# Gather operations issued from inside the mixer's step loop, with four more row buffers lent until the spread starts

## The chip, the cores and the metric

The kernel runs on one core of a Trainium2 chip. The metric is the device time of one execution in microseconds (us), given as the median of several runs. PE is the matrix engine (TensorE), DVE the vector engine, ACT the scalar engine, POOL is GpSimd, which here mainly issues indirect DMAs, and SP is the sync engine, which issues most plain DMAs.

## The reference

One layer of a decoder, 1024 tokens of 1024 channels: a mixer of three branches, then a feed-forward layer of product-key experts (PEER), then a norm.

```python
h = rms_norm(x, norm_mix)
proj = h @ w_in          # columns for the three branches and for the merge gates
o_sb  = stick_breaking_attention(...)     # 8 heads x 64, strictly causal
o_nsa = nsa_attention(...)                # compressed, selected and sliding branch
o_hg  = hgrn2_recurrence(...)             # 4 heads, chunks of 64
m = gm[0] * (o_sb @ w_sb) + gm[1] * (o_nsa @ w_nsa) + gm[2] * (o_hg @ w_hg)
x = x + m @ w_out

xc = rms_norm(x, norm_ffn)                # PEER, per token
qh = (xc @ w_q).reshape(T, 8, 2, 64)
s = einsum("nhad,akd->nhak", qh, sub_keys)        # 2 x 128 keys
top_s, top_i = top_k(s, 16)
best_s, pos = top_k(all 16 x 16 sums of top_s, 16)
eidx = ...                                # 8 heads x 16 of 16384 experts for each token
gate = softmax(best_s)
hpre = einsum("nd,nhkd->nhk", xc, u_tab[eidx])
act  = gate * gelu(hpre)
x = x + einsum("nhk,nhkd->nd", act, v_tab[eidx])
out = rms_norm(x, norm_final)
```

Each token needs 128 rows of u_tab and 128 rows of v_tab, each of 1024 float32.

## The kernel before, in words

**Parts.** The tokens are cut into four parts of 256. The mixer goes through them in order. It is written by a loop of steps (`while t < N + 3 or todo`). A step writes a few items of the three branches and then as many "pieces" (projections, gates, tails, routing) as keep PE's and VectorE's estimated work even; `mark()` closes it. `mark` stores the last VectorE instruction that has been written and the estimates v and p, in us, of the VectorE and PE work of the step.

**Two ways through PEER.** Parts 1 and 2 (`DENSE`) go through all 16384 experts with matmuls, after the mixer: 128 blocks of 128 experts each, whose u and v rows are read in full. Each token's gate for each expert comes from the spread: `spread_pieces` builds one-hot rows (`hot`, VectorE), multiplies them (`gb`, PE) and evicts the product with ACT into a staging tile of 128 x 128 x 16 float32, from which ACT's queue stores it to `d_G`. Two of the three staging tiles are the two halves of `stages`, 2 x 8 KB of each partition.

Parts 0 and 3 go through gathers. They are four tiles of 128 tokens. `gather_tile` does for each of its tiles: load of the tile's h2 row, indices and gates; 128 times an indirect DMA on POOL's queue (L1149, one u row for each of the 128 partitions, 512 KB) and a VectorE operation that multiplies it with h2 and sums it into a column of `hpre` (L1151, `u`); gelu; load of the residual row into `gacc`; 128 times an indirect DMA of a v row (L1159) and a VectorE multiply-add into `gacc` (L1161); the last norm and the store. That makes 1024 gathers.

**Buffers.** Part 0's gathers use the buffers of tag "rows", RB = 5 of 4 KB for each partition. The h2 row takes one of them, and the `gacc` row one when its turn comes. (During part 0 of the mixer the raw weights use the same five.) Part 3's gathers add space of the mixer that is free by then (`late_rows`; `rr_u`, `rr_v` in the profile).

**What sets the order.** The program is written first, and a scheduler then orders the instructions of each engine: the ones that can run by its estimates, in order of their priority, which is the order in which they were written. In the kernel before, `gather_tile` is called at the very end of the program, behind the dense stage. So a gather is behind everything else that can run. The buffers of a tag are given out in the order in which they come free in that schedule. Two things pull the gathers forward: their DMAs go to POOL, which has little else to do, and their VectorE operations are written under `paced()`, which issues each of them right behind the VectorE instruction of a certain mark. `paced` gives 420 gathers (`PACE`) to the steps from number 135 (`PACE0`) on, in proportion to p + 3.0 (`PB`); all others come behind the last mark.

The plain loads (weights, `gacc`, `h2`) are issued by SP in one queue in order; a load that waits for its buffer holds the ones behind it.

## Time and profile before

| | before |
|---|---|
| median of 3 runs | 3502.45 us (3502.05 to 3503.18) |
| profiled execution | 3511.97 us, its span 3510.2 us |
| PE busy | 3199.7 us (91%) |
| VectorE busy | 3000.6 us (85%) |
| ACT busy | 1556.4 us (44%) |
| POOL busy | 1361.7 us (39%) |
| moved by DMA | 1058.00 MB, mean 301 GB/s |
| mean TensorE clock granted | 0.942 |
| first gather issued | 579.8 us |
| first matmul of the spread | 1216.9 us |

Busy time is the time in which an engine executed something; a share is that over the span. Where rows give "duration min/median/max, first and last start", times are in us from the start of the span and durations in ns. In the listing of waits a row names the engine, the instruction that stood idle, what released it, and then the idle time in all, the number of times and the longest, in us. Rows of DMAs give the time from issue to landing. In a row of windows "(x95)" behind a busy time counts instructions. The executions of this profile and of the timed runs are different ones: the profiled one took 9.5 us longer than the median.

### The profile page before, as it was taken

How to read it: one execution, taken by the hardware profiler on the slowest of the kernel's cores; microseconds unless marked ns; L12 is line 12 of the kernel's file. 1: busy time of each engine (PE TensorE's matmuls, PEld its weight loads, DVE VectorE, ACT ScalarE, POOL GpSimd, SP SyncE). 2: the span in 40 equal slices, each digit the busy share in tenths (PEclk: the TensorE clock that was granted, in tenths of full speed). 3: DMA queues.
4: the chain of work that ended last, by engine and by line, in shares of the span. 5: the costliest groups of instructions: out<-in, count | busy, mean ns of one | idle time of the engine just before them, and what ended most of it. 6: DMA issues, size and time to landing. Idle time of an engine off the chain costs nothing.

```text
span 3510.2 us, 56907 instructions
## 1 busy us (share of the span) xinstructions
PE 3199.7 (91%) x20564; PEld 2175.3 (62%) x20564; DVE 3000.6 (85%) x6666; ACT 1556.4 (44%) x3181; POOL 1361.7 (39%) x1170
## 2 busy tenths in 40 slices
PE   7999889999997799999887889889999999999998
PEld 6887777778886688888565745434444444444443
DVE  6665679888789879889997869999988998998998
ACT  5776455554543554554455233333333333333333
POOL 0000002443332322333231334357765565676672
PEclk9999999999997799999688999989999999999999
DMA  8964856889976588897574998789999999999995
GB/s 305 334 248 147 308 185 226 320 314 310 358 284 231 199 289 291 327 332 259 191 250 154 344 372 312 241 271 387 392 384 329 385 367 362 362 368 375 367 358 219
DMA packets 359283, 1058.00 MB, mean 301 GB/s; under 512 B 35236, under 2 KB 107573, under 8 KB 354391
## 3 DMA queue, kind: packets, MB, share of 16 engines
q0 software_dynamic: 147456, 536.94, 42.5%
q1 hardware_dynamic: 206934, 483.87, 38.7%
q10 hardware_dynamic: 4608, 33.56, 2.5%
q8 instruction: 161, 2.64, 0.3%
q14 instruction: 124, 1.01, 0.1%
HBM read 944.13 MB, written 110.10 MB: 300 GB/s over the span
## 4 chain that ended last, share of the span: by engine, by line
PE 49%; DVE 23%; DMA 11%; issue 8%; ACT 6%; POOL 2%; SPq 0%; DVEq 0%; POOLq 0%; ACTq 0%
PE g L265 13%; PE acc L1441 10%; PE pj_mg L265 4%; DVE u L1151 3%; DVE gacc L1161 3%; PE g L1441 3%; DMA u<-in_peer_u_dram,gidx 3%; PE pj_r_hg L265 2%; DMA v<-in_peer_v_dram,gidx 1%; PE pb L265 1%; DMA gt<-d_G 1%; PE pj_wo L265 1%; POOL v L1159 1%; PE z_sb L417 1%; DMA vraw<-in_peer_v_dram 1%
## 5 line engine op out<-in xcount | busy, mean ns | idle before, releaser
L1159 POOL DMA_INDIRECT v<-in_peer_v_dram,gidx x421 | 556.0, 1321 | 674.0 <-DVE gacc L1161 348.4
L1149 POOL DMA_INDIRECT u<-in_peer_u_dram,gidx x417 | 529.7, 1270 | 596.6 <-DVE u L1151 367.4
L265 PE MATMUL g<-h,us 128*128 128x512 f16 x3072 | 688.2, 381 | 14.8 <-ACT ge L1400 12.1
L1441 PE MATMUL acc<-vs,ac 128*128 128x512 f16 x2304 | 542.2, 383 | 39.9 <-ACT vs L220 23.5
L1441 PEld LDWEIGHTS <-ac 128*128 128x128 f16 x3072 | 303.1, 99 | 426.1 <-issue 66.8
L1161 DVE SCALAR_TENSOR_TENSOR gacc<-v,act,gacc 128x1024 f32<-128x1024 f32 x421 | 538.9, 1280 | 29.4 <-DMA v<-in_peer_v_dram,gidx 25.8
L265 PEld LDWEIGHTS <-us 128*128 128x128 f16 x3072 | 301.6, 98 | 383.0 <-issue 21.1
L1151 DVE SCALAR_TENSOR_TENSOR u<-u,gh 128x1024 f32<-128x1024 f32 x417 | 501.9, 1219 | 33.2 <-DMA u<-in_peer_u_dram,gidx 32.7
L1400 ACT ACTIVATE ge<-g 128x512 f32<-128x512 f32 x128 | 76.1, 596 | 520.7 <-PE g L265 500.1
L265 PE MATMUL pj_mg<-hT,w_mg 128*128 128x256 f16 x2304 | 273.8, 275 | 4.0 <-ACT mg L885 4.0
L265 PEld LDWEIGHTS <-w_mg 128*128 128x128 f16 x2304 | 228.2, 100 | 33.6 <-issue 6.6
L1441 PE MATMUL g<-vs,ac 128*128 128x512 f16 x768 | 190.5, 388 | 11.6 <-ACT ge L1400 11.6
L1149 POOL DMA_INDIRECT rr_u<-in_peer_u_dram,gidx x95 | 134.2, 1413 | 96.7 <-DVE rr_u L1151 49.8
L221 DVE SCALAR_TENSOR_TENSOR vs<-vraw,vs 128x1024 f16<-128x1024 f32 x128 | 154.1, 1219 | 18.6 <-ACT vs L220 18.5
L221 DVE SCALAR_TENSOR_TENSOR us<-uraw,us 128x1024 f16<-128x1024 f32 x128 | 156.1, 1219 | 10.4 <-ACT us L220 10.3
L265 PE MATMUL pb<-o,w_b 128*128 128x256 f16 x1152 | 144.7, 281 | 21.1 <-DVE sg L923 15.1
L1159 POOL DMA_INDIRECT rr_v<-in_peer_v_dram,gidx x90 | 123.0, 1367 | 102.2 <-DVE gacc L1161 81.4
L220 ACT ACTIVATE vs<-vraw 128x1024 f16<-128x1024 f32 x128 | 131.0, 1046 | 55.0 <-DMA vraw<-in_peer_v_dram 55.0
L220 ACT ACTIVATE ac<-ge 128x512 f16<-128x512 f32 x128 | 79.9, 628 | 168.3 <-DVE ge L1434 139.0
L1434 DVE TENSOR_TENSOR ge<-ge,gt 128x256 f32<-128x256 f32 x256 | 98.4, 422 | 58.7 <-ACT ge L1400 44.9
L1223 PE MATMUL gb<-hot 128*128 128x128 f16 x512 | 125.7, 294 | 24.3 <-ACT stage L1226 13.1
L220 ACT ACTIVATE us<-uraw 128x1024 f16<-128x1024 f32 x128 | 134.2, 1048 | 21.4 <-PE g L265 12.8
(1146 smaller groups left out, 6353.8 us busy)
## 6 DMA issues: line engine op xcount, KB each, us to landing
uraw<-in_peer_uT_dram SPq DMA_DIRECT2D x128, 512.0 KB, 7.7
vraw<-in_peer_v_dram SPq DMA_DIRECT2D x128, 512.0 KB, 7.2
w_mg<-dw SPq DMA_DIRECT2D x72, 512.0 KB, 5.8
gt<-d_G SPq DMA_DIRECT2D x32, 1024.0 KB, 17.5
d_G<-stages ACTq DMA_DIRECT2D x20, 1024.0 KB, 5.9
w_r_hg<-dw SPq DMA_DIRECT2D x36, 512.0 KB, 5.4
w_b<-dw SPq DMA_DIRECT2D x72, 256.0 KB, 5.5
wr_mg<-in_wblk_dram SPq DMA_DIRECT2D x24, 512.0 KB, 5.3
```

The costliest lines, as they stand in the source:

```text
L220: S.activation(hi, src, AF.Copy, scale=scale)
L221: V.scalar_tensor_tensor(lo, in0=src, scalar=scale, in1=hi, op0=ALU.mult, op1=ALU.subtract)
L265: P.matmul(ps, l[:, k, :], r[:, k, :], start=(i == 0), stop=(i == n - 1))
L417: P.matmul(x["z"], qz[:, hh, tl * 128:(tl + 1) * 128], st["k"][:, r0 + c0:r0 + c1], start=True, stop=(c0 > 0))
L1149: G.indirect_dma_start(out=ur, out_offset=None, in_=a["peer_u"], in_offset=bass.IndirectOffsetOnAxis(ap=idx[:, c:c + 1], axis=0))
L1151: V.scalar_tensor_tensor(ur, in0=ur, scalar=1.0, in1=h2, op0=ALU.mult, op1=ALU.mult, accum_out=hpre[:, c:c + 1])
L1159: G.indirect_dma_start(out=vr, out_offset=None, in_=a["peer_v"], in_offset=bass.IndirectOffsetOnAxis(ap=idx[:, c:c + 1], axis=0))
L1161: V.scalar_tensor_tensor(acc, in0=vr, scalar=act[:, c:c + 1], in1=acc, op0=ALU.mult, op1=ALU.add)
L1223: P.matmul(ps[:, n, :], hs[:, 0, :, n], hs[:, 2, :, n], start=True, stop=False)
L1400: S.activation(ge, ps, AF.Gelu, scale=1.0 / (SW * SH2))
L1434: V.tensor_tensor(gv, gv, gt[:, :, i % 8, :], op=ALU.mult)
L1441: P.matmul(ps, ac[:, x, t * 128:(t + 1) * 128], v[:, y, dh * 512:(dh + 1) * 512], start=start and n == 0, stop=stop and n == 2)
```

## The change

The generator `gather_rows` holds the whole list of gathers: `gather_tile` now yields behind each of them. The step loop calls `gather_due()` behind each `mark()`. From step 135 on it adds 0.19 * (p + 3.0) (the new `PACE`) to the gathers owed and writes those that have come due into the program, as soon as the routing of part 0 is written. So their priority is that of the step. Their VectorE operations stand behind the VectorE instruction of the mark just made, and the old table of `paced` is gone. `seen[0]` is moved on, so that the estimates v and p leave the gathers out. What is left of the list at the program's end is written there, as before.

`lent_rows` gives part 0's gathers their buffers: of each eight in a row, the first four take a "rows" buffer as before and the next four a quarter of `stages` (4 KB of each partition), which stands idle until the spread. The first piece of the spread sets `lent[1]`, and from then on all take "rows" buffers. The profile and the listings below show a gather in lent space under the name `stages`.

```diff
@@ -23,7 +23,7 @@
 
 RPE, RDVE, REND, PD = 3.5, 3.0, 5.0, 1.2
 
-PACE0, PACE, PB = 135, 420, 3.0
+PACE0, PACE, PB = 135, 0.19, 3.0
 
 TP, LEAD = 3, 3
 
@@ -1114,30 +1114,22 @@
         total_[:] = load_["DVE"], load_["PE"]
         marks.append((next(i for i in reversed(nc.cur_bb.bb.instructions) if i.engine == mybir.EngineType.DVE), v, p))
 
-    paces = []
-
     def paced():
 
-        if not paces:
-            def rows(tau):
-                return [tau * (p + PB) if k >= PACE0 else 0.0 for k, (_, v, p) in enumerate(marks)]
-
-            lo, hi = 0.0, 10.0
-            for _ in range(40):
-                mid = (lo + hi) / 2
-                lo, hi = (mid, hi) if sum(rows(mid)) < PACE else (lo, mid)
-            acc = 0.0
-            for m, r in zip(marks, rows(lo)):
-                acc += r
-                paces.extend([m[0]] * (int(acc) - len(paces)))
-            paces.append(marks[-1][0])
-            paces.append(0)
-        k = paces[-1]
-        paces[-1] += 1
-        return tc.issue_after(paces[min(k, len(paces) - 2)])
+        return tc.issue_after(marks[-1][0])
+
+    lent = [0, False]
+
+    def lent_rows(name):
+
+        j = lent[0] % 8
+        lent[0] += 1
+        if j < 4 or lent[1]:
+            return rows(name)
+        return stages[:, j // 2 - 2, j % 2 * 64:j % 2 * 64 + 64].rearrange("p a b -> p (a b)")
 
     def gather_tile(ti):
-        row = late_rows if ti // 2 == PARTS[-1].i else rows
+        row = late_rows if ti // 2 == PARTS[-1].i else lent_rows
         h2 = load(rows(f"gh2_{ti}"), d_h2[ti])
         idx = load(gat.tile([128, 128], I32, tag="gidx", name=f"gidx_{ti}", bufs=1), d_idx[ti])
         gate = load(gat.tile([128, 128], F32, tag="ggate", name=f"ggate_{ti}", bufs=2), d_gate[ti])
@@ -1149,6 +1141,7 @@
             G.indirect_dma_start(out=ur, out_offset=None, in_=a["peer_u"], in_offset=bass.IndirectOffsetOnAxis(ap=idx[:, c:c + 1], axis=0))
             with paced():
                 V.scalar_tensor_tensor(ur, in0=ur, scalar=1.0, in1=h2, op0=ALU.mult, op1=ALU.mult, accum_out=hpre[:, c:c + 1])
+            yield
         with tc.high_priority():
             S.activation(act, hpre, AF.Gelu)
             log_exp()
@@ -1159,12 +1152,33 @@
             G.indirect_dma_start(out=vr, out_offset=None, in_=a["peer_v"], in_offset=bass.IndirectOffsetOnAxis(ap=idx[:, c:c + 1], axis=0))
             with paced():
                 V.scalar_tensor_tensor(acc, in0=vr, scalar=act[:, c:c + 1], in1=acc, op0=ALU.mult, op1=ALU.add)
+            yield
         with tc.high_priority():
             log_exp()
         y = rms_scale(acc, f"fin{ti}", rows(f"sqf{ti}"), "g")
         gf = load(rows(f"gf{ti}"), a["norm_final"].to_broadcast([128, D]))
         V.scalar_tensor_tensor(acc, in0=acc, scalar=y, in1=gf, op0=ALU.mult, op1=ALU.mult)
         nc.sync.dma_start(out[ti * 128:(ti + 1) * 128, :], acc)
+
+    def gather_rows():
+
+        for pt in PARTS:
+            if pt not in DENSE:
+                for tl in range(pt.nt):
+                    yield from gather_tile(pt.ti0 + tl)
+
+    stream = gather_rows()
+    owed = [0.0, 0]
+
+    def gather_due():
+
+        if len(marks) > PACE0:
+            owed[0] += PACE * (marks[-1][2] + PB)
+        if routed[0].done:
+            while owed[1] < int(owed[0]):
+                owed[1] += 1
+                next(stream)
+            seen[0] = len(nc.cur_bb.bb.instructions)
 
     found = {}
 
@@ -1212,6 +1226,7 @@
         def four(q):
             n0 = pt.t0 - TD + q * 4
             if q % 4 == 0:
+                lent[1] = True
                 u = n0 // 16 % 3 if n0 < TH - 32 else 2
                 stage[0] = per.tile([128, 128, 16], F32, tag="stage", name=f"stage{n0}") if u == 2 else stages[:, u]
             sp = spread[pt.i][:, :, q * 4:q * 4 + 4]
@@ -1381,6 +1396,7 @@
                 account()
         todo = [p for p in todo if not p.done]
         mark()
+        gather_due()
         t += 1
     mixing[0] = False
 
@@ -1472,10 +1488,8 @@
         V.scalar_tensor_tensor(y, in0=y, scalar=r, in1=gfd, op0=ALU.mult, op1=ALU.mult)
         nc.sync.dma_start(out[TD + t * 128:TD + (t + 1) * 128, :], y)
 
-    for pt in PARTS:
-        if pt not in DENSE:
-            for tl in range(pt.nt):
-                gather_tile(pt.ti0 + tl)
+    for _ in stream:
+        pass
 
 
 
```

Three places show how it moves instructions. In them `u0_5` is the u gather number 5 of tile 0.

POOL's queue at the first gathers, before (u0_ are buffers of tag "rows"; the MEMSETs belong to the mixer):

```order
L1149 DMA u0_0_32618<-in_peer_u_dram,gidx_0_32611 128x1024
L1149 DMA u0_1_32621<-in_peer_u_dram,gidx_0_32611 128x1024
L1149 DMA u0_2_32624<-in_peer_u_dram,gidx_0_32611 128x1024
L1149 DMA u0_3_32627<-in_peer_u_dram,gidx_0_32611 128x1024
L1149 DMA u0_4_32630<-in_peer_u_dram,gidx_0_32611 128x1024
L651 MEMSET zz_ns1g1t0b1h0_8621 128x8
L1149 DMA u0_5_32633<-in_peer_u_dram,gidx_0_32611 128x1024
L1149 DMA u0_6_32636<-in_peer_u_dram,gidx_0_32611 128x1024
L1149 DMA u0_7_32639<-in_peer_u_dram,gidx_0_32611 128x1024
L1149 DMA u0_8_32642<-in_peer_u_dram,gidx_0_32611 128x1024
L651 MEMSET zz_ns1g1t1b2h0_9212 128x8
L1149 DMA u0_9_32645<-in_peer_u_dram,gidx_0_32611 128x1024
```

Now:

```order
L1141 DMA u0_0_7357<-in_peer_u_dram,gidx_0_7350 128x1024
L1141 DMA u0_1_7360<-in_peer_u_dram,gidx_0_7350 128x1024
L1141 DMA u0_2_7363<-in_peer_u_dram,gidx_0_7350 128x1024
L1141 DMA u0_3_7366<-in_peer_u_dram,gidx_0_7350 128x1024
L1141 DMA stages_219<-in_peer_u_dram,gidx_0_7350 128x1024 x4
L1141 DMA u0_8_7377<-in_peer_u_dram,gidx_0_7350 128x1024
L651 MEMSET zz_ns1g1t0b1h0_8748 128x8
L1141 DMA u0_9_7414<-in_peer_u_dram,gidx_0_7350 128x1024
L1141 DMA u0_10_7473<-in_peer_u_dram,gidx_0_7350 128x1024
L1141 DMA u0_11_7476<-in_peer_u_dram,gidx_0_7350 128x1024
L1141 DMA stages_219<-in_peer_u_dram,gidx_0_7350 128x1024 x2
L651 MEMSET zz_ns1g1t1b2h0_9393 128x8
```

Between the first gather and the first MEMSET stood five gathers; now there are nine, four of them into lent space, and before the second MEMSET fourteen instead of nine.

SP's queue around the load of `gacc` for tile 0 (w_wo are the weights of part 1's output projection, the others weights and rows of part 2), before:

```order
L255 DMA w_q_sb1_2_11614<-dw0_1_1823 128x2048
L255 DMA w_v_sb1_2_11643<-dw0_9_1857 128x2048
L255 DMA w_i_hg2_2_11688<-dw0_33_1589 128x2048
L100 DMA gacc_0_33005<-d_x2_0_185 128x1024
L946 DMA d_x2_2_187<-x2_1_0_11120 128x1024
L946 DMA d_x2_3_188<-x2_1_1_11122 128x1024
L255 DMA w_r0_hg2_2_11734<-dw0_29_1652 128x2048
```

Now:

```order
L255 DMA w_wo0_1_11431<-dw0_63_5442 128x2048
L255 DMA w_wo1_1_11497<-dw0_64_5476 128x2048
L255 DMA w_wo2_1_11560<-dw0_65_5544 128x2048
L100 DMA gacc_0_11780<-d_x2_0_185 128x1024
L255 DMA w_wo3_1_11610<-dw0_66_5588 128x2048
L907 DMA d_g0_217<-mg0_2_10998 128x1536
L255 DMA w_wo4_1_11657<-dw0_67_5638 128x2048
L375 DMA v_sb1_2_12032<-d_v1_182 128x512
```

The load stood behind all weights of the output projection and now stands between w_wo2 and w_wo3. It waits for the VectorE operation that last used its buffer: that of u0_124 before, of u0_120 now.

VectorE ahead of `tiny_hg1_2`, the beginning of the next group of the HGRN2 branch (e_sb and r_sb belong to the stick-breaking attention), before:

```order
L1151 SCALAR_TENSOR_TENSOR u0_116_32966,hpre_0_32615<-u0_116_32966,gh2_0_32609 128x1024
L1151 SCALAR_TENSOR_TENSOR u0_117_32969,hpre_0_32615<-u0_117_32969,gh2_0_32609 128x1024
L429 SCALAR_TENSOR_TENSOR e_sb0_2_1_1_0_11094<-r_sb0_2_1_1_0_11097,e_sb0_2_1_1_0_11094 128x512
L432 TENSOR_TENSOR r_sb0_2_1_1_0_11097<-z_sb0_2_1_1_0_11093,e_sb0_2_1_1_0_11094 128x512
L429 SCALAR_TENSOR_TENSOR e_sb0_2_1_1_512_11154<-r_sb0_2_1_1_512_11156,e_sb0_2_1_1_0_11094,e_sb0_2_1_1_512_11154 128x256
L1151 SCALAR_TENSOR_TENSOR u0_118_32972,hpre_0_32615<-u0_118_32972,gh2_0_32609 128x1024
L432 TENSOR_TENSOR r_sb0_2_1_1_512_11156<-z_sb0_2_1_1_512_11153,e_sb0_2_1_1_512_11154 128x256
L1151 SCALAR_TENSOR_TENSOR u0_119_32975,hpre_0_32615<-u0_119_32975,gh2_0_32609 128x1024
L769 TENSOR_SCALAR tiny_hg1_2_11215<-raw_hg1_2_9274 128x256
```

Now:

```order
L429 SCALAR_TENSOR_TENSOR e_sb0_2_1_1_512_11463<-r_sb0_2_1_1_512_11465,e_sb0_2_1_1_0_11401,e_sb0_2_1_1_512_11463 128x256
L221 SCALAR_TENSOR_TENSOR m1_10341<-sg7_1_10871,m1_10341 128x256
L1143 SCALAR_TENSOR_TENSOR u0_104_10925,hpre_0_7354<-u0_104_10925,gh2_0_7348 128x1024
L1143 SCALAR_TENSOR_TENSOR u0_105_10928,hpre_0_7354<-u0_105_10928,gh2_0_7348 128x1024
L432 TENSOR_TENSOR r_sb0_2_1_1_512_11465<-z_sb0_2_1_1_512_11462,e_sb0_2_1_1_512_11463 128x256
L1143 SCALAR_TENSOR_TENSOR stages_219,hpre_0_7354<-stages_219,gh2_0_7348 128x1024
L1143 SCALAR_TENSOR_TENSOR u0_112_11153,hpre_0_7354<-u0_112_11153,gh2_0_7348 128x1024
L1143 SCALAR_TENSOR_TENSOR stages_219,hpre_0_7354<-stages_219,gh2_0_7348 128x1024
L1143 SCALAR_TENSOR_TENSOR u0_115_11296,hpre_0_7354<-u0_115_11296,gh2_0_7348 128x1024
L1143 SCALAR_TENSOR_TENSOR u0_120_11482,hpre_0_7354<-u0_120_11482,gh2_0_7348 128x1024
L769 TENSOR_SCALAR tiny_hg1_2_11533<-raw_hg1_2_9455 128x256
```

Two gathers stood between the last two rows of e_sb and `tiny_hg`, with r_sb between them; now there are seven, and they are not in the order of their numbers: u0_104, u0_105, u0_112, u0_115 and u0_120 with two in lent space between them.

## The prediction

> **What bounds the kernel now.** I read the page first: busy shares and the 40 slices.
>
> ```profile
> span 3510.2 us, 56907 instructions
> PE 3199.7 (91%) x20564; PEld 2175.3 (62%) x20564; DVE 3000.6 (85%) x6666; ACT 1556.4 (44%) x3181; POOL 1361.7 (39%) x1170
> PE   7999889999997799999887889889999999999998
> DVE  6665679888789879889997869999988998998998
> ```
>
> TensorE and VectorE are both nearly full, so neither alone sets the end: where one waits, the other soon does. The next view cuts the span at the places that the change touches: 575 us (first gather), 1190 us (shortly before the 200th) and 2036 us (last spread step).
>
> ```profile
> core 0: us, PE busy (x) PEld busy (x) DVE busy (x) ACT busy (x) POOL busy (x), PEclk, DMA share, GB/s
> 575.00:1190.00 615.00, 545.34 (x4086) 455.78 (x4085) 537.26 (x1497) 315.25 (x780) 227.24 (x237) 0.90 0.83 292
> 1190.00:2036.00 846.00, 748.45 (x5622) 629.92 (x5621) 741.88 (x1800) 404.12 (x931) 260.01 (x246) 0.90 0.77 272
> 2036.00:3510.00 1474.00, 1391.17 (x6472) 639.82 (x6470) 1338.18 (x2142) 492.48 (x662) 865.57 (x612) 0.98 0.94 344
> ```
>
> From 575 to 1190 us PE idles 70 us and DVE 78 us of 615. After 2036 us the dense stage runs with PE 94% busy: its length is set by its matmuls, so what the mixer gains or loses ahead of it moves the end by as much. The waits, VectorE's from 575 to 1225 us and then TensorE's, say what the idle time is:
>
> ```profile
> DVE u L1151 <- DMA u<-in_peer_u_dram,gidx: 18.8, 16, 4.8
> DVE gacc L1161 <- DMA v<-in_peer_v_dram,gidx: 8.2, 9, 2.6
> DVE e_sb L429 <- ACT e_sb L424: 7.2, 5, 2.3
> PE z_sb L417 <- DVE r_sb L432: 13.1, 9, 3.9
> PE tra_sb L438 <- ACT r_sb L433: 10.3, 6, 3.7
> ```
>
> The two longest of VectorE are gathers that have not landed: 18.8 + 8.2 = 27.0 us. Why they are late follows from the gathers' own rows (u, then v; the DVE operation, the issue on POOL, the time to landing):
>
> ```profile
> L1151 DVE SCALAR_TENSOR_TENSOR u<-u,gh x128: 1195/1218/1273, 585.1 to 938.9; 128x1024 f32<-128x1024 f32 x128
> L1149 POOL DMA_INDIRECT u<-in_peer_u_dram,gidx x128: 932/938/1963, 579.8 to 928.6; - x128
> DMA to landing us min/median/max: 4.2/6.9/10.9
> L1161 DVE SCALAR_TENSOR_TENSOR gacc<-v,act,gacc x73: 1251/1279/1286, 946.9 to 1213.1; 128x1024 f32<-128x1024 f32 x73
> DMA to landing us min/median/max: 4.1/5.9/11.9
> ```
>
> 128 u gathers in 353.8 us are one per 2.8 us. Of the five row buffers one holds h2 (later the sum), so four turn, each in 11.1 us. A turn needs 1.2 us on DVE, 0.9 on POOL and 6.9 to land: 9.0 at the median, but 13.0 with the slowest landing, and the pace is uneven. The v gathers come every 3.7 us (266.2 us over 72): 14.8 us a turn, and 1.3 + 0.9 + 11.9 = 14.1 at worst. Four buffers are just too few.
>
> **The change, part by part.** It removes no operation and adds none: 1024 gathers with their DVE operations stay.
>
> (1) Eight buffers instead of four for the first 200 gathers: a turn becomes 22.3 us against 13.0 at worst, 29.6 against 14.1 in v. The DVE waits, by stretch of the same view (575 to 840, 840 to 939; then 1225 to 2036 us, where nothing is lent):
>
> ```profile
> DVE u L1151 <- DMA u<-in_peer_u_dram,gidx: 11.9, 13, 2.6
> DVE u L1151 <- DMA u<-in_peer_u_dram,gidx: 6.9, 3, 4.8
> DVE u L1151 <- DMA u<-in_peer_u_dram,gidx: 13.8, 13, 2.2
> DVE gacc L1161 <- DMA v<-in_peer_v_dram,gidx: 8.1, 6, 2.5
> ```
>
> The first 11.9 us go, and the 8.2 us of v. In the stretch of 6.9 us, the last 33 u gathers, the changed order takes gathers out of turn (u0_105, u0_112, u0_115 and u0_120 come close together, the third place shown) and the sum's buffer is claimed early, so between none and all of it goes; I take half, 3.4. Removed: 11.9 + 8.2 + 3.4 = 23.5 us of VectorE's waiting. The 13.8 + 8.1 us behind 1225 us stay.
>
> How much of it reaches the end? Here is the longest one, from the timeline, and two windows around waits:
>
> ```profile
> 870.64 1.68 POOL L1149 DMA_INDIRECT u<-in_peer_u_dram,gidx  x1 [3.85 <-DVE u L1151]
> 879.92 1.23 DVE L1151 SCALAR_TENSOR_TENSOR u<-u,gh 128x1024 f32<-128x1024 f32 x1 [4.80 <-DMA u<-in_peer_u_dram,gidx]
> 881.81 1.22 PE L417 MATMUL z_sb<-k_sb,qz 128*128 128x512 f32 x1 [3.86 <-DVE r_sb L432]
> 664.00:676.00 12.00, 12.00 (x95) 9.82 (x92) 9.48 (x24) 4.71 (x13) 5.55 (x6) 1.00 0.72 242
> 862.00:882.00 20.00, 16.12 (x142) 14.16 (x140) 14.63 (x30) 8.42 (x23) 5.81 (x5) 0.99 0.91 317
> ```
>
> The 4.80 us on DVE became 3.86 us on PE, a share of 0.80. The wait of 1.2 us at 672 us cost PE nothing (12.00 us busy of 12.00). So the share lies between 0 and 0.80; below 0 it cannot be, since VectorE's order is nearly kept. I take 0.45, a little over the middle, because PE's two longest waits are this same chain, r_sb on DVE and ACT. 23.5 x 0.45 = 10.6 us.
>
> (2) The order. Both programs have 200 gathers consumed at nearly the same place of VectorE's list, and as many before the dense stage; moving 1.2 us of DVE work a few rows costs nothing while the other rows are ready, and at most what a late row costs PE. That happens at one place: the load of gacc, the first tile's sum row, which now stands ahead of w_wo3 in SP's queue and waits for the DVE operation of u0_120, which stands just ahead of tiny_hg.
>
> ```profile
> 914.56 0.28 DVE L769 TENSOR_SCALAR tiny_hg<-raw_hg 128x256 uint32<-128x256 f32 x1
> L265 PE MATMUL pj_wo<-m,w_wo x192: 269/273/273, 901.0 to 929.1; 128*128 128x256 f16 x192
> L255 SPq DMA_DIRECT2D w_wo<-dw x8: 319/320/320, 890.3 to 914.7; - x8
> DMA to landing us min/median/max: 3.8/6.5/7.4
> ```
>
> If it falls at 914.6 us as before, w_wo3 to w_wo7 and all loads behind them issue after that, and w_wo3 lands at 914.6 + 6.5 = 921.1. PE reached its fourth block at 901.0 + 3 x 28.1/8 = 911.5: 9.6 us lost. If VectorE is earlier by what it no longer waits (11.9 + 3.4 = 15.3 us), u0_120 is done at 899.3, ahead of the 905.0 that w_wo3 needs, and nothing is lost. Between 0 and 9.6 I take 1.4, near the lower end, which the arithmetic favours.
>
> (3) The lent space is written by ACT from the first spread step, which now waits for gathers 197 and 198, later 199 and 200:
>
> ```profile
> 1208.45 1.27 DVE L1161 SCALAR_TENSOR_TENSOR gacc<-v,act,gacc 128x1024 f32<-128x1024 f32 x1
> 1213.06 1.27 DVE L1161 SCALAR_TENSOR_TENSOR gacc<-v,act,gacc 128x1024 f32<-128x1024 f32 x1
> L1223 PE MATMUL gb<-hot x8: 277/296/301, 1216.9 to 1222.0; 128*128 128x128 f16 x8
> L1226 ACT ACTIVATE stages<-gb x8: 578/597/602, 1218.1 to 1253.3; 128x512 f32<-128x512 f32 x8
> ```
>
> Gather 198 is the one at 1208.45, gather 201 that at 1213.06. ACT first writes at 1218.1, so 8 us cover the wait; behind it in ACT's queue stand evictions that PE needs, so without that cover each us late is a us lost. Cost 0.
>
> (4) More gathers in flight beside the weights. Both kinds share 16 DMA engines, here from 575 to 1190 us:
>
> ```profile
> q0 software_dynamic: 28515, 103.84, 48.9%
> q1 hardware_dynamic: 24903, 74.98, 33.4%
> w_mg<-dw SPq DMA_DIRECT2D x30, 512.0 KB, 6.6
> 884.84 10.72 PE pj_mg L265 x96
> ```
>
> PE never waits long for a weight there, and a block lasts 10.72/4 = 2.7 us, so four blocks of lead are 10.7 us against 6.6 to land. The number of bytes is unchanged; a landing would have to grow by 4 us. I take 0; the upper bound is one such excess at a burst, some 2 us. The Trainium skill (DMA: Bandwidth & Descriptors, SWDGE vs HWDGE vs iDMA) says that each engine takes turns between its queues and that gathers and plain loads use different ones. By that a deeper gather queue would not stand ahead of a weight, which also gives 0; no run here has shown it yet.
>
> **Sum.** 10.6 - 1.4 = 9.2 us. The span becomes 3510.2 - 9.2 = 3501.0. The profiled execution took 3511.97 us, 1.8 more than its span, and the median of the three runs is 3502.45, so 3502.45 x (3511.97 - 9.2)/3511.97 = 3493.3 us.
>
> **Rivals.** (a) No gain: DVE arrives earlier and waits for ACT and PE instead, as at 672 us, where PE had no hole to close. For it: the e_sb and r_sb waits remain, and PE and DVE are equally full. Against it: the 3.86 us. Time 3502.5. The same comes out if the waits are not a matter of the ring: with the shortest landing, 4.2 us, a turn is 6.3 of 11.1 us, four buffers are enough and more give nothing. The Trainium skill (DMA: Bandwidth & Descriptors, Anatomy of one DMA) leans to that: 2.0 us plus the bytes at 436 GB/s, an estimate of 3.2 us for these 512 KB. The trace's median of 6.9 us does not agree.
>
> (b) The gain is as large as the one traced wait: 0.80 x 23.5 = 18.8 us and no cost at gacc, 3483.7. For it: the gathers' waits and PE's r_sb waits are close in size. Against it: the window at 664 us.
>
> (c) Slower: the hold of SP's queue by the gacc load. It decides if u0_120's operation comes later than 905.0 us. Then PE loses up to 9.6 us at w_wo3. The same late u0_120 closes a run of seven gathers ahead of tiny_hg, where two stood: 5 x 1.3 = 6.5 us more that the hg step waits. 9.6 + 6.5 - 0.45 x (11.9 + 8.2) = 7.1 us lost: 3509.5. For it: loads behind a waiting load on SP cannot pass it, and 28 us of blocks hang on them. Against it: the 15.3 us that VectorE should have gained by then.
>
> (d) That the change does not do what it says is nearly excluded: half of the first 200 gathers write the lent space.
>
> **How the numbers follow.** Forecast 0.38 (3488 to 3496), (b) 0.12, (a) 0.31 (from 3496 to 3509), (c) 0.19. About 0.2%, 7 us, is what a measurement of this kernel can tell from no change: under 3495.4 is faster, over 3509.5 slower. Forecast and (b) are faster together: 0.50; (a) is the same: 0.31; (c) is slower: 0.19. The range runs from a little under (b) to a little over (c), 3479 to 3514.
>
> **What would show it.** In the changed profile VectorE's waits for u and v between the first gather and the first spread step should add up to 7 us or less instead of 27.0, and those after it to about 22. The first spread step's matmuls (1216.9 us now) should come some 9 us earlier, and the dense stage should keep its length. If the waits go and the spread starts at the same time, (a) holds. If PE waits at pj_wo for w_wo with SP held by DVE u, (c) holds. The forecast is wrong from the ground if the gather waits stay: then the number of buffers was not their cause.

## The result: 1 % slower, and the profile after

The changed kernel takes 3539.19 us at the median (3536.43 to 3542.36) against 3502.81 us of the kernel before, a ratio of 1.0104 with a 95 % interval of 1.0086 to 1.0121. On another chip, where some of the variants below ran, the ratio was 1.0101 (1.0076 to 1.0126). The forecast was 3493.3 us in a range of 3479 to 3514. It is wrong, and wrong in sign.

The windows of the changed kernel, cut at the first gather, at the first and at the last matmul of the spread (us and length; busy time of each engine; then the granted TensorE clock, the busy share of the DMA engines and GB/s):

```profile
span 3534.8 us, 56919 instructions
PE 3202.2 (91%) x20564; PEld 2176.4 (62%) x20564; DVE 3003.8 (85%) x6666; ACT 1570.8 (44%) x3193; POOL 1372.6 (39%) x1170
580.50:1221.80 641.30, 558.72 (x4235) 467.31 (x4236) 561.26 (x1531) 334.62 (x822) 241.69 (x245) 0.90 0.80 288
1221.80:2052.30 830.50, 734.52 (x5444) 618.72 (x5442) 717.11 (x1750) 396.04 (x895) 253.59 (x238) 0.89 0.77 269
2052.30:3534.80 1482.50, 1389.06 (x6469) 638.22 (x6467) 1338.61 (x2143) 492.40 (x663) 868.39 (x613) 0.98 0.94 342
```

The same cuts in the kernel before, in the execution of the prediction and in a second one (e5 below):

```profile
579.80:1216.90 637.10, 564.40 (x4238) 473.47 (x4239) 559.01 (x1531) 324.14 (x813) 236.33 (x244) 0.89 0.82 289
1216.90:2036.40 819.50, 725.68 (x5441) 609.49 (x5440) 716.47 (x1750) 392.19 (x892) 251.33 (x239) 0.90 0.78 275
2036.40:3510.20 1473.80, 1390.77 (x6469) 639.42 (x6467) 1338.18 (x2142) 492.08 (x661) 865.17 (x612) 0.98 0.94 344
```

```profile
577.90:1207.90 630.00, 554.46 (x4238) 467.25 (x4239) 559.79 (x1534) 324.01 (x814) 236.59 (x245) 0.91 0.82 293
1207.90:2027.70 819.80, 726.45 (x5440) 611.35 (x5440) 714.91 (x1750) 392.89 (x892) 255.50 (x239) 0.90 0.78 274
2027.70:3493.90 1466.20, 1387.68 (x6469) 638.54 (x6467) 1337.09 (x2142) 492.16 (x662) 872.88 (x611) 0.98 0.94 346
```

All three stages grew: the first, in which the buffers are lent, from 637.1 or 630.0 to 641.3 us, the second by 11 and the third by 9 to 16. PE's busy time in the three is 2682.3 us, against 2680.9 and 2668.6; most of what grew is the time in which it stands idle, 272.0 us against 249.6 and 247.4. And yet the waits that the change was to remove did shrink. VectorE's waits for gathers in the changed kernel, 575 to 1225 us, and PE's for r_sb:

```profile
DVE stages L1143 <- DMA stages<-in_peer_u_dram,gidx: 8.5, 5, 4.8
DVE u L1143 <- DMA u<-in_peer_u_dram,gidx: 2.7, 6, 1.0
PE z_sb L417 <- DVE r_sb L432: 13.9, 8, 6.6
```

They are 11.2 us instead of 27.0, and the v gathers wait no longer at all. From issue to use a gather now has 16 to 21 us (median of each twenty, the first hundred) where it had 8.4 to 9.1. The ring of eight does its work, and the kernel is slower. The longest of PE's waits for r_sb grew from 3.9 to 6.6 us. Here is its place on VectorE:

```profile
873.24 1.21 DVE L429 TENSOR_TENSOR_SCAN e_sb<-r_sb,e_sb 128x512 f32<-128x512 f32 x1
879.25 1.23 DVE L1143 SCALAR_TENSOR_TENSOR stages<-stages,gh 128x1024 f32<-128x1024 f32 x1 [4.80 <-DMA stages<-in_peer_u_dram,gidx]
880.74 0.69 DVE L432 TENSOR_TENSOR r_sb<-z_sb,e_sb 128x512 f32<-128x512 f32 x1
897.72 1.22 DVE L1143 SCALAR_TENSOR_TENSOR u<-u,gh 128x1024 f32<-128x1024 f32 x1
898.86 1.22 DVE L1143 SCALAR_TENSOR_TENSOR u<-u,gh 128x1024 f32<-128x1024 f32 x1
```

on POOL:

```profile
824.56 0.95 POOL L1141 DMA_INDIRECT u<-in_peer_u_dram,gidx  x1 [0.87 <-DVE u L1143]
845.38 0.93 POOL L1141 DMA_INDIRECT u<-in_peer_u_dram,gidx  x1 [1.37 <-DVE nmx_ns2g0t0b1h L675]
866.60 0.94 POOL L1141 DMA_INDIRECT u<-in_peer_u_dram,gidx  x1 [3.29 <-DVE u L1143]
870.61 1.87 POOL L1141 DMA_INDIRECT stages<-in_peer_u_dram,gidx  x1 [3.07 <-DVE m L221]
```

and on PE:

```profile
874.68 0.33 PE L447 MATMUL ov_sb<-v_sb,aT_sb 128*128 128x64 f32 x2
881.57 2.05 PE L417 MATMUL z_sb<-k_sb,qz 128*128 128x512 f32 x2 [6.56 <-DVE r_sb L432]
893.56 0.69 PE L438 MATMUL tra_sb<-packed,r_sb 128*128 128x128 f32 x2 [3.53 <-ACT r_sb L433]
```

The gather used at 879.25 us was issued only at 870.61 and landed 8.6 us later, in spite of eight buffers. The order of the rows tells why, with the semaphores in the trace, which pair each gather with its use. u0_104 and u0_105, issued at 824.56 and 845.38 us, are used at 897.72 and 898.86 us, and u0_112 is used 39 us after its issue at 862.21 us. So three of the four row buffers hold rows that no one asks for yet. Three of the four lent ones do so too: rows issued at 828.1, 838.5 and 849.5 us are used at 870.5, 884.1 and 881.3 us. Two buffers of eight still turn, and the gathers in POOL's queue wait for those two (3.29 and 3.07 us at the last two lines shown). That is the out-of-turn order of the third place shown.

### The profile page after: what moved, and what is told of

It reads as the page before. It is cut to its first block, busy times and chain, and to the rows that moved or that the text cites. A ratio compares the mean times of both kernels' runs of the same rounds, so it can differ in the third digit from the quotient of the medians.

```text
span 3534.8 us, 56919 instructions
## 1 busy us (share of the span) xinstructions
PE 3202.2 (91%) x20564; PEld 2176.4 (62%) x20564; DVE 3003.8 (85%) x6666; ACT 1570.8 (44%) x3193; POOL 1372.6 (39%) x1170
## 4 chain that ended last, share of the span: by engine, by line
PE 41%; DVE 29%; DMA 13%; ACT 9%; issue 7%; POOL 1%; SPq 0%; DVEq 0%; ACTq 0%; POOLq 0%
PE g L265 7%; PE acc L1457 6%; DVE gacc L1154 5%; PE pj_mg L265 4%; DVE u L1143 3%; DMA gt<-d_G 3%; PE pj_r_hg L265 2%; DMA vraw<-in_peer_v_dram 2%; DMA u<-in_peer_u_dram,gidx 2%; PE pj_wo L265 2%; PE g L1457 1%; PE pb L265 1%; DVE vs L221 1%; DVE us L221 1%; DVE rr_u L1143 1%
## 5 line engine op out<-in xcount | busy, mean ns | idle before, releaser
L1152 POOL DMA_INDIRECT v<-in_peer_v_dram,gidx x385 | 509.9, 1324 | 663.3 <-DVE gacc L1154 363.8
L1141 POOL DMA_INDIRECT u<-in_peer_u_dram,gidx x353 | 463.2, 1312 | 484.3 <-DVE u L1143 283.7
L1457 PE MATMUL acc<-vs,ac 128*128 128x512 f16 x2304 | 543.9, 383 | 45.5 <-ACT vs L220 22.5
L1154 DVE SCALAR_TENSOR_TENSOR gacc<-v,act,gacc 128x1024 f32<-128x1024 f32 x385 | 493.4, 1282 | 19.0 <-DMA v<-in_peer_v_dram,gidx 15.4
L1143 DVE SCALAR_TENSOR_TENSOR u<-u,gh 128x1024 f32<-128x1024 f32 x353 | 425.1, 1220 | 23.1 <-DMA u<-in_peer_u_dram,gidx 22.9
L1141 POOL DMA_INDIRECT rr_u<-in_peer_u_dram,gidx x95 | 144.9, 1526 | 82.4 <-DVE rr_u L1143 44.0
L221 DVE SCALAR_TENSOR_TENSOR us<-uraw,us 128x1024 f16<-128x1024 f32 x128 | 156.2, 1220 | 10.6 <-ACT us L220 10.5
L265 PE MATMUL pb<-o,w_b 128*128 128x256 f16 x1152 | 141.4, 278 | 22.5 <-DVE sg L923 15.5
```

The costliest lines, as they stand in the source:

```text
L221: V.scalar_tensor_tensor(lo, in0=src, scalar=scale, in1=hi, op0=ALU.mult, op1=ALU.subtract)
L265: P.matmul(ps, l[:, k, :], r[:, k, :], start=(i == 0), stop=(i == n - 1))
L1141: G.indirect_dma_start(out=ur, out_offset=None, in_=a["peer_u"], in_offset=bass.IndirectOffsetOnAxis(ap=idx[:, c:c + 1], axis=0))
L1143: V.scalar_tensor_tensor(ur, in0=ur, scalar=1.0, in1=h2, op0=ALU.mult, op1=ALU.mult, accum_out=hpre[:, c:c + 1])
L1152: G.indirect_dma_start(out=vr, out_offset=None, in_=a["peer_v"], in_offset=bass.IndirectOffsetOnAxis(ap=idx[:, c:c + 1], axis=0))
L1154: V.scalar_tensor_tensor(acc, in0=vr, scalar=act[:, c:c + 1], in1=acc, op0=ALU.mult, op1=ALU.add)
```

## The experiments

Each ratio is against the kernel before on the same chip. "Stage 1" is the time from the first gather to the first matmul of the spread, and "waits" VectorE's waits for gathers from 575 to 1225 us, both from the run's profiled execution, as is the number of table loads on ACT.

| kernel | ratio (95 % interval) | stage 1 us | waits us | table loads |
|---|---|---|---|---|
| before (two executions) | 1 | 637.1, 630.0 | 27.0, 28.6 | 91 |
| the change | 1.0104 (1.0086 to 1.0121) | 641.3 | 11.2 | 103 |
| e6 the change again | 1.0101 (1.0076 to 1.0126) | 645.3 | 15.4 | 103 |
| e1 no lent space | 1.0048 (1.0025 to 1.0072) | 629.2 | 22.5 | 93 |
| e2 in number order | 1.0081 (1.0064 to 1.0097) | 637.1 | 6.0 | 109 |
| e3 lowest priority | 1.0042 (1.0024 to 1.0060) | 638.8 | 8.2 | 101 |
| e4 gacc by POOL | 1.0072 (1.0049 to 1.0095) | 642.0 | 10.7 | 103 |
| e7 before, 416 paced | 1.0077 (1.0054 to 1.0099) | 625.1 | 25.9 | 90 |
| e8 before, 424 paced | 1.0037 (1.0025 to 1.0050) | 638.6 | 33.0 | 96 |
| e9 one sigmoid group held | 1.0083 (1.0062 to 1.0105) | 638.8 | 14.9 | 95 |
| e10 all groups held | 1.0146 (1.0121 to 1.0171) | 640.2 | 13.4 | 90 |
| e11 before, groups held | 1.0057 (1.0037 to 1.0076) | 624.2 | 29.4 | 87 |
| e12 in order, low, held | 1.0156 (1.0125 to 1.0187) | 636.9 | 7.3 | 94 |
| **e13 old order, lent** | **0.9973 (0.9959 to 0.9987)** | 617.6 | 2.3 | 91 |
| e14 old order, three buffers | 1.0178 (1.0154 to 1.0201) | 676.3 | 92.2 | 91 |
| e15 order of e1, lent | 1.0015 (1.0000 to 1.0031) | 616.8 | 2.0 | 93 |
| e16 old order, 7 more loads | 0.9998 (0.9985 to 1.0012) | 633.3 | 30.4 | 98 |
| e17 order of the change, gathers in turn | 1.0064 (1.0047 to 1.0081) | 634.6 | 2.4 | 103 |

### Undoing parts: e1 to e4

e1, without the lent space:

```diff
-        if j < 4 or lent[1]:
-            return rows(name)
-        return stages[:, j // 2 - 2, j % 2 * 64:j % 2 * 64 + 64].rearrange("p a b -> p (a b)")
+        return rows(name)
```

> The change without the lent space: every gather of part 0 takes a row buffer, and the gathers are still written into the steps. Theory A (the eight buffers work, and what loses time is the changed order of the queues, which comes from writing the gathers into the steps): still slower than before, 3520 to 3545 us, and VectorE's waits for gathers between 575 and 1225 us are back at about 27 us. Theory B (more gathers in flight crowd out other work): the loss goes with the lent space, 3500 to 3507 us.

e1 takes 3522.32 us: slower than before, with most of the waits back (22.5 us), as theory A said. But half of the change's loss is gone with the lent space, and stage 1 is 12 to 16 us shorter than the change's although its waits are 7 to 11 us longer. At this point it looked as if waits for gathers were not on the path at all (theory F below).

e2, each gather's VectorE operation queued behind the one before it, beside the mark (shortened; the definition of `turn` is left out):

```diff
-        return tc.issue_after(marks[-1][0])
+        return turn()      # issue_after(marks[-1][0]) and issue_after(the gather before)
```

> The change, with each gather's VectorE operation also queued behind that of the gather before it, so that no gather is taken out of turn (27 of the first 200 are). Theory A1 (gathers taken out of turn hold their buffers and with them POOL's queue, and that is the loss up to 1220 us): the PE hole of 6.6 us near 880 us and VectorE's wait of 4.8 us ahead of it go, the spread starts 5 to 10 us earlier, 3525 to 3533 us. If the order among gathers is not the cause: 3535 to 3545 us.

e3, the lowest priority:

```diff
-                next(stream)
+                with tc.high_priority(offset=-1000000):
+                    next(stream)
```

> The change, with the gathers written at the same places but at the lowest priority, as in the kernel before, where they were written last. If the priority of their step lets gathers go ahead of mixer work that is ready (theory A2): 3505 to 3515 us. If priority is not the cause, since the row behind which each gather stands is the same: 3535 to 3545 us.

e4, the load of `gacc` taken off SP's queue:

```diff
-        acc = load(rows(f"gacc_{ti}"), d_x2[ti])
+        acc = rows(f"gacc_{ti}")
+        G.dma_start(acc, d_x2[ti])
```

> The change, with the residual row (gacc) loaded through POOL's queue instead of SP's, so that no weight stands behind it. If the hold of SP's queue costs what the prediction's rival (c) said: up to 9.6 us less than the change, 3529 to 3535 us. If it costs nothing, as PE's unbroken pj_wo blocks from 910.5 us on suggest: 3536 to 3542 us.

The medians of e2 and e4, 3534.94 and 3536.34 us, lie close to those of the change (3536.45 and 3539.19), and their intervals overlap its own. e3 halves the loss without reaching what was expected of it. e2 does what theory A1 said up to the spread, which begins at 1217.0 us, 5 to 8 us earlier than in the change; but its dense stage lasts 1493.0 us instead of 1480 to 1483, and the time is not the one expected. For e4 the changed kernel's own trace is clearer than the ratio: the load is issued at 907.7 us and PE runs its 192 pj_wo matmuls from 910.5 us on with no wait for a weight among its waits. Rival (c)'s hold of SP's queue did not happen. The trouble with e2 and e3 is that each of these edits gives the scheduler another problem, and it moves rows all over the program. So the next question was what a fresh ordering costs by itself.

### What a fresh ordering costs: e5 to e8

e5 and e6 are the kernel before and the change once more. e7 and e8 are the kernel before with one number altered by 1 %:

```diff
-PACE0, PACE, PB = 135, 420, 3.0
+PACE0, PACE, PB = 135, 416, 3.0     # e8: 424
```

> The kernel before, unchanged, for a second trace. If one trace can be compared with another stage by stage, its first spread matmul, last spread matmul and end lie within 2 us of the first trace's 1216.9, 2036.4 and 3510; if the executions scatter by stage, the stage that scatters shows here.

> The changed kernel, unchanged, on the chip on which the variants run. Against the kernel before 1.008 to 1.011. Its trace loses about 10 us near 880 us, stands 5 us late at the first spread matmul and 16 us late at the last, if these are properties of the order and not of one execution.

> The kernel before with 416 gathers paced into the mixer instead of 420: same mechanism, same buffers, four gathers fewer in 1900 us, but a fresh ordering (1305 of some 5560 VectorE rows move; the change moves 1381). Theory D (any fresh ordering costs, because the order before was chosen for its time): 3515 to 3540 us, slower than before by as much as the change without lent space. Theory A (writing the gathers into the steps is what costs): within 0.2% of before, 3502 to 3515 us.

> The same with 424 gathers paced. Theory D: 3515 to 3540 us here too, though the amount may differ from that with 416. Theory A: 3502 to 3515 us.

e5: 3495.72 us, its trace 16.3 us shorter than the first, 7 us of it in stage 1 and 7.6 in the dense stage. So differences of less than some 8 us between two single traces mean nothing in these stages. The change's own two traces repeat: first spread matmul at 1224.5 us (1221.8), last at 2050.5 (2052.3).

e7 and e8 are the turn of the study. Four gathers more or fewer in 1900 us, with the same buffers and the same mechanism, cost 0.8 and 0.4 %. The places of e7's loss are elsewhere (its stage 1 is short, its dense stage 1500.6 us against 1473.8 and 1466.2). So a change of this kernel that moves some 1000 of 5560 VectorE rows has to reckon with a loss of 0.4 to 0.8 % that has nothing to do with what it is meant to do, as far as these two edits show it, and theory D stands.

Part of this loss is not idle time. All kernels here run the same 20564 matmuls on PE, but not at the same granted TensorE clock. The profile pages of e5, e7 and e8:

```profile
span 3493.9 us, 56907 instructions
PE 3186.5 (91%) x20564; PEld 2169.8 (62%) x20564; DVE 2998.3 (86%) x6666; ACT 1556.9 (45%) x3181; POOL 1373.9 (39%) x1170
```

```profile
span 3525.0 us, 56914 instructions
PE 3208.5 (91%) x20564; PEld 2177.6 (62%) x20564; DVE 3001.6 (85%) x6666; ACT 1554.1 (44%) x3180; POOL 1355.9 (38%) x1170
```

```profile
span 3525.3 us, 56940 instructions
PE 3207.7 (91%) x20564; PEld 2179.1 (62%) x20564; DVE 3001.2 (85%) x6666; ACT 1563.9 (44%) x3186; POOL 1372.1 (39%) x1170
```

The mean granted clock is 0.947 in e5, 0.942 in the first execution of the kernel before (PE busy 3199.7 us) and 0.939 in e7 and e8. PE stands idle (span less busy time) for 307.4 us in e5, 310.5 in the first execution, 316.5 in e7 and 317.6 in e8. So only 6 to 10 us of what e7 and e8 lose in these traces is waiting; 8 to 22 us are the same matmuls taking longer at a lower clock. It is not a matter of one execution: the mean clock of all timed runs is 0.941 for e7, e8 and the change and 0.945 for the kernel before on the same chip. Why the clock is lower under these orders no run shows.

### A cause that did not hold: table loads, e9 to e12, e16

The change has 12 more table loads on ACT than the kernel before, which the prediction had not counted. They gather where a group of sigmoids (L902) has its last input late: the attention's Exp and Ln steps run in between, and each loads a table. ACT in the changed kernel, at the hole in PE shown above:

```profile
885.36 1.28 ACT L902 ACT_TABLE_LOAD   x1
887.61 1.28 ACT L423 ACT_TABLE_LOAD   x1
889.86 1.28 ACT L424 ACT_TABLE_LOAD   x1
891.80 1.28 ACT L433 ACT_TABLE_LOAD   x1
```

There are nine between 885 and 914 us, where the kernel before has two. e9 holds this one group together, e10 all of them, e11 does that in the kernel before, e12 together with e2 and e3 (shortened):

```diff
-            S.activation(st["mg"][:, i], ps, AF.Copy, scale=PS)
+            st["last"] = S.activation(st["mg"][:, i], ps, AF.Copy, scale=PS)
...
-                tc.keep_in_program_order(S.activation(o, x, AF.Sigmoid))
+                with tc.issue_after(mg[0]["last"].ins):      # e9: only for head 1 of part 2
+                    tc.keep_in_program_order(S.activation(o, x, AF.Sigmoid))
```

> The change, with one thing ordered: in the one group of sigmoids near 885 us (head 1 of part 2) each sigmoid is issued behind the last eviction of the merge gates (mg, L885), which the group's last sigmoid reads, so that the group runs in one piece. 95 function-table loads instead of 103, and few rows move beside that. Theory E (the window between the first and the last sigmoid of a group is filled with Exp and Ln steps of the attention, and each of these loads a table of 1.28 us in the attention's chain): the 9 loads between 885 and 914 us become 2 to 4, PE's waits there shrink, the first spread matmul comes 8 to 12 us earlier than the change's 1221.8 to 1224.5 us, and the time is 3522 to 3530 us. Theory D alone (any fresh ordering, no single cause): 3530 to 3545 us.

> The change, with all groups of sigmoids held together in the same way: 90 table loads instead of 103. Theory E: the losses near 885, 1107 and 1301 us go, the stage from the first gather to the first spread matmul lasts 632 us or less (641 and 645 in the change), and the time is 3508 to 3522 us. Theory D alone: 3520 to 3545 us.

> The kernel before with the groups of sigmoids held together: 87 table loads instead of 91, none of them in a long window. Theory E: within 0.3% of before, 3495 to 3510 us, since there is little to remove. Theory D: a fresh ordering (693 rows of VectorE move), 3512 to 3530 us.

> The change with gathers in number order, at the lowest priority, and the groups of sigmoids held together: 94 table loads. If lending is worth what the prediction said once the order does not spoil it (10.6 us): the stage from the first gather to the first spread matmul lasts 622 to 627 us and the time is 3490 to 3500 us. If waits for gathers are not on the path (theory F, after the variants without lent space, which had 22 to 33 us of these waits and the shortest stages): 628 to 636 us, and 3505 to 3525 us.

In e9 two loads are left at the place and the first spread matmul comes at 1217.1 us, 5 to 7 us earlier than in the change, but its time, 3531.58 us, misses what theory E asked for. e10 to e12 are slower than their bases (the change for e10 and e12, the kernel before for e11) although their loads are fewer; e11 lies where theory D put it, e10 and e12 above all that was expected. In these three the first gather is issued only at 590.6 to 592.6 us instead of 578 to 581, presumably because holding the early groups delays part 0. None of these settles what a load costs, since all are fresh orderings. That needed a kernel with the old order.

### The order held fixed: e13 to e16

From the scheduled kernel before, the order of every instruction of VectorE, TensorE, ACT and SP was written down as a list of numbers, and a kernel was made that chains its instructions in this order, one behind the other (shortened):

```diff
+    for e in ENGINES:                     # DVE, PE, Activation, SP
+        seq = ...                         # the order written down
+        own = [... instructions of engine e: the others first, then the gathers' ...]
+        for p, q in zip(seq[:-1], seq[1:]):
+            tc.add_manual_dep(own[q], own[p].name, ..., reason="order")
```

`paced()` and `keep_in_program_order` are left out there, since the list replaces them, and so is the table preload (`log_exp`) behind the v gathers of a tile (in e15 and e17 only behind those of part 3). The base is the changed kernel; so the gathers of e13 use the lent space, while every row of the four engines stands where it stood before the change. The traces bear this out: VectorE's 6666 rows, PE's 20564 matmuls and ACT's 3181 rows follow each other as in the kernel before. On POOL, which was left free, 14 of 1170 rows stand elsewhere. (Lines are counted 13 higher in this kernel, L1156 is the u operation.) e14 and e16 use the same list without the lent space, e15 the list of e1 with it.

> The lent buffers with the order of the kernel before: VectorE, TensorE, ACT and SP run the same rows in the same order as in the kernel before (none of 5564 VectorE rows differs), the gathers write the lent space, and nothing else of the change is left. The prediction's part (1) (waits for gathers reach the end at a share of 0.45, 23.5 us of them go): 8 to 13 us less than before, 3488 to 3494 us. Theory F (those waits are not on the path): within 0.15% of before, 3496 to 3506 us. Theory B (more gathers in flight crowd out other transfers): 3510 us or more.

> The order of the kernel before on the same four engines, and one row buffer kept out of use during tile 0's 256 gathers, so that three turn instead of four. A turn of 9.0 us at the median (1.2 on VectorE, 0.9 on POOL, 6.9 to land) for three gathers is 3.0 us for each, above the 2.8 us of the pace in u. Waits of VectorE for gathers between 575 and 1225 us rise from 27 to 29 us to 60 us or more. If they reach the end at a share of 0.45: 15 us or more slower, 3515 us and up. Theory F: 3500 to 3510 us.

> The order of the variant without lent space (e1) on the same four engines, with the lent buffers. It has e1's 93 table loads. Part (1) of the prediction: 8 to 13 us less than e1, 1.0012 to 1.0025 times before. Theory F: as e1, 1.0035 to 1.006. If lending itself costs what the change and e1 differ by: 1.008 or more.

> The order of the kernel before on the same four engines, four turning buffers, and three switches of ACT's function table put in ahead of attention steps near 890 us; with what they force, 7 more table loads of 1.28 us (98 instead of 91), as the change has 9 near 885 us where the kernel before has 2. Theory E (they stand in the attention's chain, for which TensorE waits): 6 to 10 us slower than before, 3507 to 3512 us, the loss standing in the trace from about 900 us on. If ACT, busy 44% of the time, hides them: within 3 us of before.

e13 takes 3493.93 us against 3505.14, 0.9973: 11.2 us by the medians and 5 to 14 by the interval. It beats both kernels. PE's idle time is 299.6 us, 8 to 11 less than in the kernel before, and the mean clock of the timed runs is the same for both, 0.944. The first two windows of e13 and then its waits for gathers:

```profile
578.50:1196.10 617.60, 554.09 (x4239) 467.59 (x4240) 560.05 (x1535) 323.89 (x814) 242.12 (x246) 0.91 0.83 299
1196.10:2011.60 815.50, 726.35 (x5441) 610.76 (x5440) 713.85 (x1748) 392.53 (x892) 253.97 (x237) 0.90 0.78 274
```

```profile
DVE gacc L1167 <- DMA v<-in_peer_v_dram,gidx: 1.2, 3, 0.5
DVE stages L1156 <- DMA stages<-in_peer_u_dram,gidx: 0.7, 1, 0.7
DVE u L1156 <- DMA u<-in_peer_u_dram,gidx: 0.4, 1, 0.4
```

25 to 26 us of waits went, and stage 1 became 12.4 to 19.5 us shorter: a share of 0.5 to 0.8. e15 says the same with another order: 1.0015 against e1's 1.0048. e14 says it from the other side. Its waits:

```profile
DVE u L1157 <- DMA u<-in_peer_u_dram,gidx: 69.1, 43, 5.6
DVE gacc L1168 <- DMA v<-in_peer_v_dram,gidx: 23.1, 15, 3.1
```

92.2 us, 64 to 65 more than with four buffers; stage 1 lasts 676.3 us, 39 to 46 more, a share of 0.6 to 0.7, and the time is 59.6 us longer, more than these waits. Tile 0's last gathers run in the stage of the spread, where the waits grow too (38.8 us against 24.8), and the granted clock was 0.939. Theory F, which e1 had suggested, falls: the waits are on the path. Theory B falls too. With up to eight in flight the u gathers of part 0's first tile land in 7.6 us at the median (6.9 before) and the v gathers up to the spread in 5.8 (5.9 before).

e16, the old order with four buffers and seven more loads near 890 us, takes 3506.49 us, 0.9998 (0.9985 to 1.0012). Theory E falls as a price: in the old order the seven loads cost nothing that can be measured. What the loads cost in the order of the change, where they stand beside PE's hole, was not tried. e16 also shows that chaining the instructions gains nothing by itself: its rows on VectorE and PE are those of e13, its waits for gathers are 30.4 us, and it is as long as the kernel before. The Trainium skill (ScalarE: Activation LUTs, What ACT_TABLE_LOAD costs) gives about 1283 ns for the load and about 1380 ns for a drain, 2.66 us for every switch, which would be an estimate of 18.6 us for these seven. The trace shows the 1.28 us, and the next operation begins right behind it (a load at 887.61 us and an Exp at 888.90 in the change); no run here shows the drain.

### Which rows: e17

e17 has the order of the change on the four engines, row for row, except that the gathers take their places on VectorE in the order of their numbers. (POOL's queue follows them.)

> The order of the change on VectorE, TensorE, ACT and SP, row for row, with one thing changed: the places of gathers on VectorE are kept, and the gathers take them in the order of their numbers. If gathers taken out of turn are what spoils the ring (u0_104 and u0_105 hold their buffers for over 50 us, a later gather is issued at 870.6 us and VectorE waits 4.8 us for it): VectorE's waits for gathers up to 1225 us fall from 11 to 15 us to under 6, and the time is 5 to 10 us less than the change's, 1.007 to 1.0085 times before. If they also cost TensorE's other holes of that stretch: 1.005 or less. If the places of the mixer's rows alone cost: 1.009 to 1.011.

Its ratio is 1.0064, against 1.0101 for the change: the gathers out of turn cost 0.4 %, some 13 us (2 to 23 by the two intervals), where 5 to 10 were expected. The waits, and PE's row at the place of the hole:

```profile
DVE gacc L1167 <- DMA v<-in_peer_v_dram,gidx: 2.2, 2, 1.1
DVE stages L1156 <- DMA stages<-in_peer_u_dram,gidx: 0.2, 1, 0.2
873.30 1.10 PE L430 MATMUL z_sb<-k_sb,qz 128*128 128x512 f32 x2 [1.65 <-DVE r_sb L445]
```

The waits are 2.4 us, and PE's hole of 6.56 us is 1.65. The trace shows the place: PE's matmuls come in the same order in both kernels, and between 860 and 900 us those of e17 gain 8 to 9 us on the change. They are 9 to 11 us ahead at the last spread matmul. This execution, the slowest of e17's six (3538.33 us), loses that again in its dense stage (1495.3 us against 1482.5), so the 13 us rest on the timed runs. The rest of the way to e13, 0.9 % or about 32 us, is the order of the other rows and the places of the gathers among them: the same operations but for 12 table loads, the same buffers, 2.4 and 2.3 us of waits for gathers. One such place can be read. TensorE in e13, where the change stands idle for 6.56 us:

```profile
863.23 1.02 PE L430 MATMUL z_sb<-k_sb,qz 128*128 128x512 f32 x2
864.59 10.64 PE L278 MATMUL pj_mg<-hT,w_mg 128*128 128x256 f16 x96
875.07 0.60 PE L430 MATMUL z_sb<-k_sb,qz 128*128 128x256 f32 x2
```

and in the change, the same two steps of the attention, the next one and the first projection block:

```profile
865.31 1.08 PE L417 MATMUL z_sb<-k_sb,qz 128*128 128x512 f32 x2
870.07 0.60 PE L417 MATMUL z_sb<-k_sb,qz 128*128 128x256 f32 x2
881.57 2.05 PE L417 MATMUL z_sb<-k_sb,qz 128*128 128x512 f32 x2 [6.56 <-DVE r_sb L432]
885.92 2.78 PE L265 MATMUL pj_mg<-hT,w_mg 128*128 128x256 f16 x24
```

In e13 four projection blocks stand between the two steps, 10.64 us of matmuls without a wait. In the change the first block comes behind both steps and the next one, at 885.92 us, so that PE has nothing to run while r_sb is late. Nearly the same stretch of work in e13 and in the change (matched by its first and last matmuls; 1230 and 1194 matmuls):

```profile
775.00:920.00 145.00, 141.73 (x1230) 124.60 (x1228) 132.06 (x333) 71.41 (x191) 60.85 (x59) 1.00 0.96 353
```

```profile
782.00:947.80 165.80, 144.72 (x1194) 124.55 (x1192) 133.79 (x336) 83.40 (x205) 59.42 (x62) 0.95 0.86 306
```

PE is busy for nearly as long in both (141.73 and 144.72 us, at a granted clock of 1.00 and 0.95); the change takes 20.8 us more. The gathers out of turn have their part in it, and that PE's order alone would cost the rest was not tried.

## Why the prediction was wrong

**Part (1), the buffers: right in mechanism and size.** It put the gain at 10.6 us, from 23.5 us of waits and a share of 0.45. With the order held, 25 to 26 us went and 11.2 us reached the end (e13, 5 to 14 by the interval). The second pair, e15 against e1, gives 11.6 us by the ratios (2 to 21 by the intervals). The share of 0.45 is 0.43 to 0.45 at the end by the medians; in stage 1 it was 0.5 to 0.8. That the middle of a range as wide as 0 to 0.80 was hit so closely is in part luck.

**Part (2), the order: the step that failed.** It said that moving gathers "a few rows costs nothing while the other rows are ready", and looked for a price only at SP's queue, 1.4 us. The order cost about 45 us (1.0101 against 0.9973; 35 to 55 by the intervals): some 13 for gathers out of turn, some 32 for the order of all other rows. In the traces 31 to 33 us of it are idle time of PE (332.6 and 330.6 us in the change, 299.6 in e13), and 9 to 12 us are the same matmuls at a lower clock (0.941 against 0.944). Why the order of the other rows costs that much is read at one place only and stays open beyond it. The sentence of part (1) that the share cannot be below 0, "since VectorE's order is nearly kept", rests on the same step: the difference in order counted gathers ahead of a point and not where PE's filling work stood against the steps that wait. 1381 of some 5560 VectorE rows were moved, and in the trace 823 of PE's 20564 matmuls stand more than 40 places from where they stood. The words "removes no operation and adds none" were wrong too, by 12 table loads; seven such loads cost nothing in the old order (e16).

**The out-of-turn stretch.** The prediction saw it (6.9 us of waits, half of them kept) and priced it as waits alone. Waits of 11.2 us stayed in all, not 3.5. By e17 the gathers out of turn cost some 13 us in all. Buffers that are held back also hold POOL's queue, and TensorE had nothing to run there.

**Part (3), the lent space's end: right.** The first spread step waits for nothing there; ACT first writes the lent space at 1222.9 us, 6.8 us after its last gather began on VectorE (1216.1 us, 1.3 us long).

**Part (4), crowding: right in its price, not in its landings.** The w_wo weights of part 1 land in 10.3 us at the median in the change instead of 6.5, nearly the 4 us that the prediction named as the limit; those of w_mg stay at 6.5. PE's waits for weights between 575 and 1225 us are still 0.2 us in all (1.5 in e6), and e13 with eight in flight, where w_wo lands in 7.5 us, is the fastest kernel.

**The rivals.** (a) had the waits gone and PE waiting for ACT and VectorE instead; PE's waits of that kind are there, but the mechanism that (a) named, no hole to close, is refuted by e13. (b)'s share of 0.80 is above what reached the end. (c) had the right sign with the wrong place: PE did not wait for w_wo; the row of gathers ahead of tiny_hg did exist, and tiny_hg came earlier all the same, at 906.2 us instead of 914.6. No rival said that the order of the other rows would change all over the program and that this has a price.

**What would have shown it.** The prediction asked for gather waits of 7 us or less, the first spread matmul 9 us earlier and an unchanged dense stage. The first came near (11.2), the second failed (4.9 us later), and the third failed by 8.7 us. For the dense stage the cause stays open: PE idles 93 us there in the change and 79 to 83 in the kernel before, behind late `vs` and `ge` tiles, and single executions differ by 7.6 us.

## What to carry to other kernels

Where a scheduler orders the program, an edit has two prices: that of its mechanism, and that of the fresh ordering. Measure the second by an edit that means nothing (a pacing number by 1 %): if it costs 0.4 to 0.8 %, as it did here, no mechanism worth 0.3 % can be judged from a rebuilt kernel. To judge the mechanism, chain the instructions in the old order and change the buffers alone; here that turned a loss of 1 % into a gain of 0.3 %. And compare traces by PE's idle time and by the granted clock apart, not by the span alone.

A ring deeper than before helps only while it is used in turn: a buffer whose row is used 39 to 73 us after its issue is not there, and the gathers queued behind it wait with it.

## What was not expected of the hardware

Two executions of the kernel before differed by 16.3 us in 3500. 13.2 us of that are busy time of PE for the same matmuls, 3199.7 us at a granted clock of 0.942 and 3186.5 at 0.947; its idle time differed by 3.1 us only. Seven table loads of 1.28 us in ACT's queue, in the midst of the attention's chain, cost nothing in the end that could be measured. And the median landing of a gather hardly depended on how many were in flight: for u 6.9 us with four buffers and 7.6 with eight (e13), for v 5.9 and 5.8, though the slowest u grew from 10.9 to 15.9.
